# A LayerNorm put behind the first matmul that reads it, and a shift taken from four tiles

## The chip, the cores and the metric

One core of a Trainium2 chip runs the whole program. The metric is device time in microseconds (us) of one execution; the median of the runs counts.

## What is computed

Three transformer blocks on a sequence of 256 tokens with 2048 features. The change touches the seam of the second block (attention) and the third (retention). Cut to that, the reference is:

```python
# attention block: x is 256 x 2048, ALPHA = 2 ** 0.5
y = attention_out @ attn_w_out                   # 2048 x 2048
x = layer_norm(ALPHA * x + y, ln_gain[0], ln_bias[0])
# retention block reads the normed x
proj = x @ ret_w_in                              # q, k, v, gate of 8 heads
...
x = layer_norm(ALPHA * x + retention_out @ ret_w_out, ln_gain[1], ln_bias[1])

def layer_norm(x, gain, bias):
    mu = mean(x); var = mean((x - mu) ** 2)      # over the 2048 features
    return (x - mu) * rsqrt(var + eps) * gain + bias
```

## The kernel before

**Layout and arithmetic.** Activations lie transposed: a tile holds 128 features by 256 tokens, and sixteen tiles hold x. TensorE (PE) multiplies in a 32-bit format of reduced precision (fp32r), so each operand is split in a high and a low half. An activation tile is 128 x 512: columns 0 to 255 (`x[:, :T]`) the high half, columns 256 to 511 the low half. Of the weights, ScalarE (ACT) makes the high half `wh` (L374) and VectorE (DVE) the low half `wl` (L387), one unit of 128 x 1024 at a time, four buffers each. `next_unit` (L391) takes the next unit at the start of its eight (m, k) steps, issues `wh` three units ahead and `wl` two units ahead. SyncE loads the weights from HBM.

**A T job** (`job_T`, L416) makes four output tiles of 128 x 256 (or two), each in a PSUM bank of its own. A step (m, k) is two products, L449 (high weights on both halves, 512 columns) and L450 (low weights on the high half, 256 columns); with `one=True` it is three of 256 columns (L446, L447, L450), and all lands in one half of the bank. After the last k of an m it calls `evac(m, ps[m])`. With `tail=2` the last two units go m by m, so that the four results come apart; with `tail=1` all four come in the last four steps. An N job (`job_N`, L455) makes results with tokens on the partitions.

**Order of the work.** The program's order on each engine is fixed when it is built. A small scheduler (`Sched`, L274) holds generators, called tasks. Each step of a job adds its nominal 325 ns (`S.adv`), and each 650 ns is a tick: a task that has yielded n is resumed n ticks later and puts its next instructions in the queues there. `S.drain(t)` puts all the rest of a task in at once. Each engine takes its queue in order.

**PSUM banks.** `st()` (L407) hands out banks in turn. During the attention output jobs there are six (four of tag `st`, and `sx0`, `sx1`); after `more_banks(pm, 0)` (L1701) there are the four of tag `st`. The first retention job takes all four, and the job behind it (values of head 0, an N job) takes the first two of the same four again.

**The seam.** Four attention output jobs mm = 0 to 3 (L1587, L1632) give tiles 4 mm to 4 mm + 3. `ev_res` (L1370) adds both halves of the result to `xr[k]`, which holds ALPHA x, and calls `LN.add(k)`. Class `LN` (L1259):
- for k < 8, POOL (GpSimd) sums the tiles to `lnc`; after tile 7 the task `shift` (L1290) takes the mean over these features from all sixteen tiles (L1297, two of three on POOL, one on DVE), first from 8 to 15, then each of 0 to 7 with its `stat`;
- `stat(k)` (L1314): ACT squares the tile (L1321), POOL adds it to a running sum (L1322), and POOL or DVE adds the square to another (L1324);
- `ev_res` drains the shift before it touches a tile k >= 8, which is at the end of job mm = 2;
- `sums` (L1339): small products that sum over the partitions; `finish` (L1346): mean, variance, reciprocal root on DVE (three steps by `rsqrt`, L488), and two products (L1359, L1367) that spread scale (`rm`) and offset over the partitions.

After job mm = 3 all tasks are drained, `finish` is run, and the task `apply0` (L1637) norms tile after tile: times scale (L1643, POOL), plus offset (L1644, DVE), times gain plus bias to the high half (L1647, ACT) and to a full copy `lny` (L1649 on POOL for odd tiles, L1651 on ACT for even ones), and the low half as their difference (L1655, DVE). The first retention job (L1691, `rqk`: q and k of head 0, `tail=1`) reads these tiles `x3[k]`, and so does every later job of the block. Its results are added up by `ev_rqk` (L1680). Then the constants `c4` are loaded by POOL's queue (L1705), and the task `task_rope` (L1748) rotates q and k beside the value job. During job mm = 1 the task `decay` (L1596) computes the decays of the eight heads, with some fifty small DVE operations. The second LayerNorm (`ln1`, L1852) uses the same class behind the retention output.

## Time and profile before

| | us |
|---|---|
| median of 3 runs | 2308.82 |
| lowest and highest | 2308.04 and 2324.27 |
| the profiled execution | 2322.28 |
| its span (first to last instruction) | 2320.5 |
| mean granted TensorE clock in it | 0.991 of full |

The timelines below are of the profiled execution, in us from the start of its span. Engines are PE (matmul), DVE (VectorE), ACT (ScalarE), POOL (GpSimd). A clock of 1.00 is 2.4 GHz, 0.50 is 1.2 GHz.

### The profile page before, as it was taken

The numbers are of one execution on the slowest core, as the hardware profiler recorded it, in microseconds if no ns is written. First come the engines' busy times: TensorE is split into PE (matmuls) and PEld (weight loads), VectorE is DVE, ScalarE is ACT, GpSimd is POOL, SyncE is SP. The second block draws the span as 40 slices with busy tenths as digits, with TensorE's granted clock in tenths as the row PEclk, the third lists the DMA queues.
The fourth block names the chain that finished last, engine by engine and source line by source line (L and its number), as shares of the span: only waits on it lengthen the run. The fifth ranks groups of instructions, "written<-read, shape, count | busy, mean of one in ns | idle before, by whom it ended". The sixth has DMA issues, their size and how long they took to land.

```text
span 2320.5 us, 33510 instructions
## 1 busy us (share of the span) xinstructions
PE 2276.0 (98%) x12755; PEld 1963.9 (85%) x12755; DVE 1532.2 (66%) x2372; ACT 1141.5 (49%) x1690; POOL 414.8 (18%) x406
## 2 busy tenths in 40 slices
PE   8999999999999999999999999999999999999997
PEld 7877888888888888888888888888888888888887
DVE  6666697655555555555558898777677676776464
ACT  5457545544443344444445556455444544446343
POOL 2224331111100011110012222650000000001061
PEclk9999999999999999999999999989999999999998
DMA  7643455565565566666555454444655555556553
GB/s 251 227 150 112 122 187 180 195 190 187 182 192 188 177 189 189 188 185 191 183 190 181 146 156 153 156 168 160 185 168 175 179 172 187 169 173 189 188 168 114
DMA packets 114657, 408.55 MB, mean 176 GB/s; under 512 B 12882, under 2 KB 15186, under 8 KB 114368
## 3 DMA queue, kind: packets, MB, share of 16 engines
q1 hardware_dynamic: 113184, 400.80, 54.9%
q0 software_dynamic: 1168, 5.53, 0.7%
q8 instruction: 100, 1.64, 0.3%
q14 instruction: 61, 0.50, 0.1%
q10 hardware_dynamic: 144, 0.08, 0.0%
HBM read 404.24 MB, written 4.21 MB: 176 GB/s over the span
## 4 chain that ended last, share of the span: by engine, by line
PE 83%; DVE 5%; POOL 3%; issue 2%; ACT 1%; DMA 0%; POOLq 0%; ACTq 0%; DVEq 0%
PE st L449 41%; PE st L450 22%; PE st L473 5%; PE st L474 4%; PE st L475 4%; DVE wl L387 2%; POOL xr L1297 1%; PE mO L1809 1%; PE st L446 1%; PE st L447 1%; PE mA L854 1%; PE mS L1782 0%; POOL lnq L1324 0%; POOL lny L1649 0%; PE mO L835 0%
## 5 line engine op out<-in xcount | busy, mean ns | idle before, releaser
L387 DVE TENSOR_TENSOR wl<-wf,wh 128x1024 fp32r<-128x1024 f32 (+1 forms) x750 | 949.5, 1275 | 301.1 <-ACT wh L374 299.8
L374 ACT ACTIVATE wh<-wf 128x1024 fp32r<-128x1024 f32 (+1 forms) x750 | 788.4, 1055 | 698.9 <-PE st L449 440.9
L449 PE MATMUL st<-xA,wh 128*128 128x512 f32 x2144 | 768.3, 402 | 8.0 <-DVE xA L514 6.7
L450 PE MATMUL st<-xA,wl 128*128 128x256 f32 x2272 | 640.5, 282 | 2.8 <-DVE wl L387 2.8
L449 PE MATMUL st<-xB,wh 128*128 128x512 f32 x1536 | 548.7, 400 | 4.6 <-DVE xB L1655 2.1
L449 PEld LDWEIGHTS st<-xA,wh 128*128 128x128 f32 x2144 | 404.4, 189 | 107.5 <-DVE xA L514 6.7
L450 PEld LDWEIGHTS st<-xA,wl 128*128 128x128 f32 x2272 | 432.0, 190 | 4.2 <-DVE wl L387 4.1
L450 PE MATMUL st<-xB,wl 128*128 128x256 f32 x1536 | 432.0, 281 | 0.0
L449 PEld LDWEIGHTS st<-xB,wh 128*128 128x128 f32 x1536 | 290.4, 189 | 75.5 <-DVE xB L1655 3.2
L450 PEld LDWEIGHTS st<-xB,wl 128*128 128x128 f32 x1536 | 291.8, 190 | 1.1
L449 PE MATMUL st<-act,wh 128*128 128x512 f32 x704 | 248.8, 399 | 0.0
L450 PE MATMUL st<-act,wl 128*128 128x256 f32 x704 | 197.7, 281 | 0.0
L474 PE MATMUL st<-wl,xB 128*128 128x512 f32 x448 | 174.8, 390 | 1.0 <-DVE wl L387 1.0
L473 PE MATMUL st<-wh,xB 128*128 128x512 f32 x448 | 175.4, 392 | 0.0
L475 PE MATMUL st<-wh,xB 128*128 128x512 f32 x448 | 174.5, 389 | 0.0
L449 PEld LDWEIGHTS st<-act,wh 128*128 128x128 f32 x704 | 132.3, 188 | 33.1
L663 DVE TENSOR_TENSOR evs<-st,evt 128x256 f32<-128x256 f32 x110 | 46.2, 423 | 149.9 <-ACT evt L661 149.8
L450 PEld LDWEIGHTS st<-act,wl 128*128 128x128 f32 x704 | 133.0, 189 | 0.0
L1210 POOL TENSOR_TENSOR evs<-evs,R 128x256 f32<-128x256 f32 x44 | 32.4, 737 | 487.3 <-DVE evs L663 487.3
L1753 POOL TENSOR_TENSOR rm<-qkr,c 128x512 f32<-128x512 f32 x16 | 32.5, 2032 | 456.7 <-DVE qkr L1687 451.7
L474 PEld LDWEIGHTS st<-wl,xB 128*128 128x128 f32 x448 | 84.2, 188 | 17.9 <-DVE wl L387 1.9
L475 PEld LDWEIGHTS st<-wh,xB 128*128 128x128 f32 x448 | 84.1, 188 | 17.8
(426 smaller groups left out, 2604.8 us busy)
## 6 DMA issues: line engine op xcount, KB each, us to landing
wf<-in_w_c SPq DMA_DIRECT2D x264, 512.0 KB, 4.2
wf<-in_w_e SPq DMA_DIRECT2D x256, 512.0 KB, 3.9
wf<-in_w_d SPq DMA_DIRECT2D x112, 512.0 KB, 3.6
wf<-in_w_a SPq DMA_DIRECT2D x84, 512.0 KB, 3.8
wf<-in_w_b SPq DMA_DIRECT2D x32, 512.0 KB, 4.0
xr<-in_xT SPq DMA_DIRECT2D x16, 256.0 KB, 5.4
wf<-in_w_a SPq DMA_DIRECT2D x5, 420.0 KB, 4.1
dr<-d POOLq DMA_DIRECT2D x1, 2048.0 KB, 9.7
```

What stands on the lines that cost most here:

```text
L374: ACT.activation(wh[q][:, :n], wf[q][:, :n], AF.Copy)
L387: V.tensor_tensor(wl[q][:, :n], wf[q][:, :n], wh[q][:, :n].bitcast(F32), OP.subtract)
L446: PE.matmul(ps[m][:, :T], hv[:, cs], x[:, :T], start=kk == 0, stop=False)
L447: PE.matmul(ps[m][:, :T], hv[:, cs], x[:, T:], start=False, stop=False)
L449: PE.matmul(ps[m], hv[:, cs], x, start=kk == 0, stop=False)
L450: PE.matmul(ps[m][:, :T], lv[:, cs], x[:, :T], start=False, stop=kk == K - 1)
L473: PE.matmul(p, xh, h[:, o:o + n], start=kk == 0, stop=False)
L474: PE.matmul(p, xh, l[:, o:o + n], start=False, stop=False)
L475: PE.matmul(p, xl, h[:, o:o + n], start=False, stop=kk == K - 1)
L663: V.tensor_tensor(s, p[:, :T], t, OP.add)
L1210: G.tensor_tensor(s, s, R2, OP.mult)
L1753: G.tensor_tensor(m, x[:, ::-1], rsn.rearrange("p (a t) -> p a t", a=2), OP.mult)
```

## The change

**The norm moves behind the first retention job.** As soon as the statistics of tile k are issued, the new task `gain(k)` makes a tile `xg[k]` of 516 columns: high half of `xr[k]` times gain (ACT), four columns `cgb[k]` with gain and bias in halves (POOL), and the low half (DVE). `rqk` of head 0 multiplies these (`ext=True`): 260, 256 and 258 columns a step, so that each result holds also the sums of the weights times gain and times bias. `head`, `sums`, `finish` and the norming of all tiles become one task `apply0`, which starts with the job and has six ticks ahead of its first product. `ev_first` drains `apply0`, and then gives scale, offset and bias to the result. All copies `lny` go to ACT; of the products with the scale four go to DVE. `sums` is called once in place of three times.

**The shift comes from four tiles** (`NS = 4`), is begun ahead of job mm = 1 (for `ln1` behind mm = 0), and yields after each subtraction; `stat` starts two ticks later and is a task of its own for each tile. `ev_res` drains the shift from k = 4 on.

**Smaller edits.** mm = 3 has no longer `one=True`, nor extra weight buffers (`alt`) for its last two units. The normed tiles lie in other buffers (`NT`, and `GT` for the tiles of 516 columns); `c4` and the rest follow.

```diff
+GT = [f"B{k}" for k in range(6, 16)] + [f"A{k}" for k in range(6)]
+NT = [f"A{k}" for k in range(6, 16)] + [f"B{k}" for k in range(6)]
...
+                if ext:
+                    PE.matmul(ps[m][:, :T + 4], hv[:, cs], x[:, :T + 4], start=kk == 0, stop=False)
+                    PE.matmul(ps[m][:, :T], hv[:, cs], x[:, T + 4:], start=False, stop=False)
+                    PE.matmul(ps[m][:, :T + 2], lv[:, cs], x[:, :T + 2], start=False, stop=kk == K - 1)
+                    if kk == K - 1:
+                        evac(m, ps[m])
+                    S.adv(340)
+                    continue
...
         def shift(self):
-            yield 6
+            yield 5
...
-            for k in [*range(8, 16), *range(8)]:
-                (V if k % 3 == 2 else G).tensor_tensor(xr[k], xr[k], self.c, OP.subtract)
-                if k < 8:
+            n = 0
+            for k in [*range(self.NS, 16), *range(self.NS)]:
+                (V if n % 3 == 2 else G).tensor_tensor(xr[k], xr[k], self.c, OP.subtract)
+                n += 1
+                yield 1
+                if k < self.NS:
+                    S.add(self.stat(k))
                     yield 2
-                    yield from self.stat(k)
...
         def stat(self, k):
+            yield 2
...
+            if self.done:
+                yield 1
+                yield from self.done(k)
...
+    def gain(k):
+
+        if k >= 10:
+            yield 4
+        x = newg(k)
+        g = lng[0][:, k:k + 1]
+        ACT.activation(x[:, :T], xr[k], AF.Copy, scale=g)
+        G.tensor_copy(x[:, T:T + 4], cgb[:, k])
+        yield 2
+        V.scalar_tensor_tensor(x[:, T + 4:], xr[k], g, x[:, :T].bitcast(F32), OP.mult, OP.subtract)
+        xg.t[k] = x
+
+    def gain_by(k):
+        xg.by[k] = S.add(gain(k))
+        if k == 15:
+            tap.append(S.add(apply0()))
+        yield 1
...
-    for mm in range(1, 4):
-        job_T(take(), og, ev_res(ln0, mm), 2, q3 if mm == 3 else None, one=mm == 3)
-    S.drain_all()
-    rm = ln0.finish()
-    x3 = XS(S)
...
     def apply0():
-        for z in range(4):
-            (G if z else V).tensor_tensor(xr[z], xr[z], rm[z > 0], OP.mult)
+
+        yield 6
+        ln0.head()
+        ln0.sums(ln0.s, ln0.q, True)
+        yield 1
+        yield from ln0.finish()
+        rm = ln0.rm
+        yield 1
+        for z in range(2):
+            G.tensor_tensor(xr[z], xr[z], rm[1], OP.mult)
         pend = []
         for k in range(16):
-            if k + 4 < 16:
-                G.tensor_tensor(xr[k + 4], xr[k + 4], rm[1], OP.mult)
+            if k + 2 < 16:
+                (V if k % 4 == 1 else G).tensor_tensor(xr[k + 2], xr[k + 2], rm[1], OP.mult)
             V.tensor_tensor(xr[k], xr[k], rm[2], OP.add)
...
+            ACT.activation(y, xr[k], AF.Identity, scale=lng[0][:, k:k + 1], bias=lnb[0][:, k:k + 1])
             pend.append((k, x, y))
-            while len(pend) > (0 if k == 15 else 1 if k < 3 else 2):
+            while len(pend) > (0 if k == 15 else 1):
...
-            yield 1 if k < 8 else 2
-
-    tap = S.add(apply0())
+            yield 1 + k % 2
+
+    ln0.begin()
+    for mm in range(1, 4):
+        job_T(take(), og, ev_res(ln0, mm), 2)
+    while len(xg.by) < 16:
+        for t in list(S.tasks):
+            S.step(t)
...
+    def ev_first(m, p):
+
+        w, s = m // 2, m % 2
+        if s == 0:
+            qkr[(0, w)] = xa_tile("qkr", (P, 2, T))
+        S.drain(tap[0])
+        gb = small(2)
+        V.tensor_reduce(gb, p[:, T:T + 4].rearrange("p (a b) -> p b a", a=2), AX.X, OP.add)
+        q = qkr[(0, w)][:, s]
+        V.tensor_tensor(q, p[:, :T], ln0.rm[1], OP.mult)
+        V.scalar_tensor_tensor(q, ln0.rm[2], gb[:, 0:1], q, OP.mult, OP.add)
+        ACT.activation(q, q, AF.Identity, bias=gb[:, 1:2])
...
-    j = take()
-    job_T(j, x3, ev_rqk(0, 0, xa_tile))
+    job_T(take(), xg, ev_first, ext=True)
...
     for mm in range(4):
         job_T(take(), og, ev_res(ln1, mm), 2, one=mm == 3)
+        if mm == 0:
+            ln1.begin()
```

## Rows read from the trace of the kernel before

**Rows 1.** The page, busy time, share of the span and instructions of each engine.

```profile
PE 2276.0 (98%) x12755; PEld 1963.9 (85%) x12755; DVE 1532.2 (66%) x2372; ACT 1141.5 (49%) x1690; POOL 414.8 (18%) x406
```

**Rows 2.** The table by stretch: the stretch and its length in us, then busy us (and instructions) of PE, its weight loads, DVE, ACT and POOL, then the granted clock, the DMA share and GB/s.

```profile
1500.00:1510.00 10.00, 6.29 (x34) 5.79 (x34) 5.33 (x4) 5.54 (x9) 9.92 (x11) 0.69 0.38 109
...
1526.48:1561.08 34.60, 29.44 (x149) 24.77 (x148) 28.19 (x61) 22.89 (x38) 22.10 (x24) 0.80 0.29 92
...
1535.60:1541.20 5.60, 5.55 (x17) 4.49 (x18) 4.03 (x8) 3.62 (x8) 5.60 (x8) 0.50 0.00 0
...
2230.00:2240.00 10.00, 9.23 (x51) 7.37 (x49) 3.72 (x3) 5.23 (x9) 8.98 (x10) 1.00 0.48 155
```

**Rows 3.** The list of waits of PE: who waited for whom, us in total, times, the longest.

```profile
PE st L446 <- ACT wh L374: 2.8, 1, 2.8
...
PE st L449 <- DVE xB L1655: 2.1, 1, 2.1
```

**Rows 4.** The timeline of PE in and behind job mm = 2: start us, us, engine, line, instruction, and in brackets the idle time before it and who ended it.

```profile
1501.64 0.28 PE L450 MATMUL st<-xA,wl 128*128 128x256 f32 x1
...
1504.69 0.58 PE L446 MATMUL st<-xA,wh 128*128 128x256 f32 x1 [2.77 <-ACT wh L374]
...
1510.65 0.31 PE L446 MATMUL st<-xA,wh 128*128 128x256 f32 x1
...
1511.03 0.28 PE L446 MATMUL st<-xA,wh 128*128 128x256 f32 x1
...
1511.39 0.28 PE L446 MATMUL st<-xA,wh 128*128 128x256 f32 x1
```

**Rows 5.** The timeline of ACT in the same stretch, same columns.

```profile
1495.63 1.04 ACT L374 ACTIVATE wh<-wf 128x1024 fp32r<-128x1024 f32 x1
...
1501.79 1.03 ACT L1321 ACTIVATE lnt<-xr 128x256 f32<-128x256 f32 x3 [1.79 <-POOL xr L1297]
...
1503.60 1.99 ACT L374 ACTIVATE wh<-wf 128x1024 fp32r<-128x1024 f32 x2
```

**Rows 6.** The timelines of PE (its first product of job mm = 1) and of DVE, during job mm = 1, and one subtraction of the shift in mm = 2.

```profile
1450.68 0.47 PE L449 MATMUL st<-xA,wh 128*128 128x512 f32 x1
...
1462.40 1.23 DVE L387 TENSOR_TENSOR wl<-wf,wh 128x1024 fp32r<-128x1024 f32 x1
...
1464.71 3.49 DVE L387 TENSOR_TENSOR wl<-wf,wh 128x1024 fp32r<-128x1024 f32 x3
...
1483.17 0.95 DVE L1297 TENSOR_TENSOR xr<-xr,lnc 128x256 f32<-128x256 f32 x1
```

**Rows 7.** The timeline of PE from the end of job mm = 3 to the first product of the first retention job.

```profile
1525.07 0.50 PE L1343 MATMUL pcs<-ones,lns 128*128 128x1 f32 x4
...
1525.88 0.36 PE L446 MATMUL st<-xA,wh 128*128 128x256 f32 x1
...
1526.20 0.28 PE L450 MATMUL st<-xA,wl 128*128 128x256 f32 x1
...
1531.45 1.22 PE L1359 MATMUL lpb<-lndg,ones 128*128 128x256 f32 x2 [3.04 <-ACT lndg L1362]
...
1532.46 1.06 PE L1367 MATMUL lpn<-lndg,ones 128*128 128x256 f32 x2
...
1535.65 0.80 PE L449 MATMUL st<-xB,wh 128*128 128x512 f32 x1 [2.12 <-DVE xB L1655]
```

**Rows 8.** The timelines of DVE (five rows) and ACT (four rows) in `finish` and `apply0`, and two rows of the table of groups from 1533.6 to 1557.2 (line, engine, operation, shapes, count, busy us, mean ns, idle us before and its releaser).

```profile
1528.45 0.16 DVE L1350 TENSOR_SCALAR sm<-pcs 128x2 f32<-128x2 f32 x1 [1.50 <-PE pcs L1343]
...
1531.00 0.29 DVE L1364 TENSOR_SCALAR lndg<-ident,sm 128x128 f32<-128x128 f32 x1
...
1546.42 0.95 DVE L1655 TENSOR_TENSOR xB<-lny,xB 128x256 fp32r<-128x256 f32 x1
...
1553.12 0.42 DVE L1655 TENSOR_TENSOR xB<-lny,xB 128x256 fp32r<-128x256 f32 x1
...
1556.77 0.43 DVE L1655 TENSOR_TENSOR xB<-lny,xB 128x256 fp32r<-128x256 f32 x1 [0.38 <-POOL lny L1649]
...
1534.11 0.60 ACT L1647 ACTIVATE xB<-xr,vec 128x256 fp32r<-128x256 f32 x1
...
1547.80 0.60 ACT L1647 ACTIVATE xB<-xr,vec 128x256 fp32r<-128x256 f32 x1 [0.79 <-DVE xr L1644]
...
1548.30 0.59 ACT L1651 ACTIVATE lny<-xr,vec 128x256 f32<-128x256 f32 x1
...
1548.80 1.05 ACT L374 ACTIVATE wh<-wf 128x1024 fp32r<-128x1024 f32 x1
...
L1655 DVE TENSOR_TENSOR xB<-lny,xB 128x256 fp32r<-128x256 f32 x16 | 9.9, 621 | 2.1 <-POOL lny L1649 1.9
...
L1643 POOL TENSOR_TENSOR xr<-xr,lnrm 128x256 f32<-128x256 f32 x12 | 9.8, 836 | 0.0
```

**Rows 9.** The timelines of DVE (the first evacuation of the first retention job) and of PE (the start of the value job, and two products of it that waited).

```profile
1559.70 0.42 DVE L1687 TENSOR_TENSOR qkr<-st,evt 128x256 f32<-128x256 f32 x1 [0.23 <-ACT evt L1686]
...
1561.08 0.40 PE L473 MATMUL st<-wh,xB 128*128 128x512 f32 x1
...
1570.12 0.50 PE L474 MATMUL st<-wl,xB 128*128 128x512 f32 x1 [0.43 <-DVE wl L387]
...
1573.74 0.50 PE L474 MATMUL st<-wl,xB 128*128 128x512 f32 x1 [0.61 <-DVE wl L387]
```

More of the change, by code (lines that the diff above doesn't have):

```diff
@@ L414, in more_banks, with job_T @@
         banks["n"] = 0
-    def job_T(j, xs, evac, tail=1, alt=None, raw=None, one=False):
+    def job_T(j, xs, evac, tail=1, raw=None, one=False, ext=False):
         K, nt, kc = len(j["rows"]), len(j["tiles"]), j["kc"]
@@ L427, in job_T @@
                 kn = min(kc, K - k0)
[L428 removed]
+                h, l = next_unit(tail > 1 and cc == nch - 1)
                 hv = h[:, :kn * nt * P].rearrange("p (k m) -> p k m", k=kn)
@@ L1260, in body, with __init__ @@
         tag = "m"
-        def __init__(self, pool, x, pair):
+        NS = 4
+        def __init__(self, pool, x, pair, done=None):
             self.base = pool
@@ L1266, in __init__ @@
             self.c, self.s, self.q = t("lnc"), t("lns"), t("lnq")
-            self.task = None
-            self.x, self.pair = x, pair
+            self.x, self.pair, self.done = x, pair, done
             self.tpre = S.add(self.pre())
@@ L1288, in pre, with begin, head @@
                 yield 1 + k % 2
+        def begin(self):
+            self.task = S.add(self.shift())
         def shift(self):
-            yield 6
+            yield 5
             pb = self.pp.tile([P, 512], F32, name="lp", tag=self.tag)
             PE.matmul(pb[:, :T], ones, self.c, start=True, stop=True)
-            ACT.activation(self.c, pb[:, :T], AF.Copy, scale=1.0 / (8 * P))
+            ACT.activation(self.c, pb[:, :T], AF.Copy, scale=1.0 / (self.NS * P))
             yield 1
-            for k in [*range(8, 16), *range(8)]:
-                (V if k % 3 == 2 else G).tensor_tensor(xr[k], xr[k], self.c, OP.subtract)
-                if k < 8:
+            n = 0
[5 more added lines that the diff above has]
+                    S.add(self.stat(k))
                     yield 2
-                    yield from self.stat(k)
         def add(self, k):
-            if k < 8:
-                if k == 0:
-                    G.tensor_copy(self.c, xr[k])
-                else:
-                    G.tensor_tensor(self.c, self.c, xr[k], OP.add)
-                if k == 7:
-                    self.task = S.add(self.shift())
-            else:
-                S.add(self.stat(k))
+            if k >= self.NS:
+                S.add(self.stat(k))
+            elif k == 0:
+                G.tensor_copy(self.c, xr[k])
+            else:
+                G.tensor_tensor(self.c, self.c, xr[k], OP.add)
+        def head(self):
+            self.ps = self.pp.tile([P, 512], F32, name="pcs", tag=self.tag)
+            for tt in range(2):
+                PE.matmul(self.ps[:, 2 + tt:3 + tt], ones, deps, start=tt == 0, stop=False,
+                          skip_group_check=True)
         def stat(self, k):
+            yield 2
             if k == 0:
@@ L1317, in stat @@
                 ACT.activation(self.q, xr[k], AF.Square)
-                return
-            if k < 14:
+            elif k < 14 or self.done:
                 sq = self.base.tile([P, T], F32, name="lnt", tag="lnt", bufs=3)
@@ L1324, in stat @@
                 (G if k < 12 else V).tensor_tensor(self.q, self.q, sq, OP.add)
-                if k == 11:
-                    self.ps = self.pp.tile([P, 512], F32, name="pcs", tag=self.tag)
-                    for tt in range(2):
-                        PE.matmul(self.ps[:, 2 + tt:3 + tt], ones, deps, start=tt == 0, stop=False,
-                                  skip_group_check=True)
+                if self.done:
+                    pass
+                elif k == 11:
+                    self.head()
                 elif k == 13:
@@ L1594, in body @@
     ln0.pools(q3, pm)
+    cgb = q3.tile([P, 16, 4], F32R, name="cgb")
+    for z, v in enumerate((lng[0], lnb[0])):
+        ACT.activation(cgb[:, :, z], v, AF.Copy)
+        V.tensor_tensor(cgb[:, :, 2 + z], v, cgb[:, :, z].bitcast(F32), OP.subtract)
     def decay():
@@ L1677, in xa_tile @@
         spare[0] += 1
-        return pxs.tile(list(shape), F32, name=name, tag=f"xA{spare[0] % 16}")
+        t = xtile(GT[spare[0] % 16], F32)
+        return t[:, :shape[1]] if len(shape) == 2 else t.rearrange("p (a t) -> p a t", a=shape[1])
+    def ev_first(m, p):
[9 more added lines that the diff above has]
+        ACT.activation(q, q, AF.Identity, bias=gb[:, 1:2])
     def ev_rqk(h, m0, mk):
@@ L1855, in body @@
         job_T(take(), og, ev_res(ln1, mm), 2, one=mm == 3)
+        if mm == 0:
+            ln1.begin()
     S.drain_all()
-    rm = ln1.finish()
+    run(ln1.finish())
+    rm = ln1.rm
     for k in range(16):
```

59 lines of the change are left out of this document (30 added, 29 removed).

## The prediction, written before the changed kernel had run

> **What bounds the kernel now.** I read the page's busy shares first: TensorE (PE) is busy nearly all of the span [rows 1], so a change is worth the time in which PE stands still or runs at its lower clock. The table by stretch [rows 2] was next, and it shows three such places in reach of this change. The list of PE's waits [rows 3] names who ended the idle time, and the timelines of PE and of the engine named [rows 4, 5, 7 to 9] give the length.
>
> Place one, in the third attention output job (mm=2): PE stops after the product at 1501.64, restarts at 1504.69, waits again, and runs at half clock until 1510.65 [rows 4]. ACT's queue made it: the weight copy behind this wait sat from 1495.63 to 1503.60 behind squares of the LayerNorm that waited for POOL [rows 5]. Place two, the norm itself: the last product of the job is at 1526.20 and ends at 1526.48 (call this E), the first product of the retention job starts at 1535.65 [rows 7], and then runs at 0.50 of the clock [rows 2]. Place three is a small copy of place one in the last LayerNorm, 2230 to 2240, PE 9.23 of 10.00 [rows 2].
>
> The reader should also see a fourth thing. In the 34.6 us from E to the second retention job DVE is busy 28.2 us and ACT 22.9 us [rows 2]. What these two do there is normalise x and split it for all later jobs. The change doesn't take this work away, it takes PE's first job out from behind it.
>
> **Place one: shift from four tiles.** PE lost from 1501.76 to 1510.65, 8.9 us, for 24 products that take 0.12 us each at full clock (three of them from 1511.03 to 1511.39): 2.9 us. So 6.0 us are lost [rows 4]. In the change the shift starts in mm=1, the sixteen subtractions are spread by one tick each, and a square is issued two ticks after its result. ACT then waits for POOL only in the tail of mm=1, where I count 15 POOL operations in some 8.5 us; at 0.84 us each [rows 8] POOL is late by 4 us at most, against the 8 us that broke it before [rows 5]. I take the whole gain: **-6.0 us** (ends 0 and -6.0).
>
> **New cost in mm=1.** DVE runs the decay task there and is already late: the low halves of units 5, 6, 7 follow in the order 1462.40 and three together at 1464.71 [rows 6]. PE starts the job at 1450.68 and takes 2.9 us a unit (eight steps of 0.36), so it wants unit 5 at 1465.1 and unit 6 at 1468.0; unit 5 is there at 1463.6, unit 6 some 1.2 us after 1464.71, at 1465.9. The slack is 1.5 and 2.1 us. Ahead of unit 6 now come three of the five DVE subtractions, at 0.43 to 0.95 us (2.0 in all at the middle) [rows 6, 8], the two small ones for the columns (0.3), and POOL beside two weight subtractions (an estimate of 0.5 each, by what the 0.43 us subtraction loses to POOL at its worst): 3.3 us against 2.1. I take **+1.2 us** (ends 0 and +3.5, the latter with a clock drop as in place one).
>
> **Sums.** Of the three calls of sums two are gone, and the one left moves behind E: **-0.8 us** before E (1525.07 to 1525.88 [rows 7]); its return is in the walk below. mm=3 goes from three 256-column products a step to one of 512 and one of 256, and the first retention job the other way round (260, 256, 258 columns): 768 columns either way but for six, so I count nothing; the ends are 0.3 us on either side.
>
> **Place two, walked from E.** The gained sums xg[0] to xg[11] are ready, so PE goes straight on. DVE still owes evacuation 15, two additions of squares, two low halves (13 and 12) and then the low half of the job's second unit: 0.9 + 4 x 0.45 + 1.1 = 3.8 us, where PE wants it at 8 x 0.36 = 2.9; PE waits 0.9. The head and sums stand at tick 7 (13 steps of 0.36 us, plus the wait): E+6, and end at E+7.2. Then DVE: thirteen small operations, 2.55 us (1528.45 to 1531.00 [rows 8]), with one low half of weights (1.1) between them, diagonal at E+11; ACT's half E+11.6; PE, which by then stands at this product, waits 0.5 and needs 0.5 (1.0 at half clock, 1531.45 to 1532.46 [rows 7]); another low half on DVE, the second diagonal, ACT's copy of the scale: E+13.5; POOL's first product and DVE's first addition: the loop over sixteen tiles begins at **E+14.8**. In the kernel before it begins at 1534.11, E+7.6 [rows 8].
>
> How long is the loop? ACT now makes both copies of each tile, 0.5 us apart (1547.80, 1548.30, 1548.80 [rows 8]): 16 x 1.0, and four weight copies of 1.05: 20.2 us is its floor. Before, the loop took 1534.11 to 1557.2, 23.1 us [rows 8]. DVE needs about 19 us, with a wait for ACT in every pair of tiles. I take 21.5, near the floor, because POOL's eight copies leave: **E+36.3**. The ends are 20.2 and 26.9 (below).
>
> On the same point the Trainium skill, SBUF — State Buffer, section Who interferes with whom, says that a DVE instruction with two SBUF inputs contends with a GpSimd instruction that reads SBUF. The trace agrees: the subtraction at L1655 takes 0.62 us on the mean beside POOL's products of 0.84 [rows 8], and 0.43 in its last copy, without them. By that rule the loop is shorter than before with eight POOL copies fewer, and the rival of a slow loop is less likely.
>
> Now who waits. The loop is paced by ticks, 1.5 a tile from tick 16, and the job has 31 before its first result: tile 10 is reached. ev_first drains the rest, tiles 11 to 15, ahead of its own operations on DVE. And the second job (values, head 0) writes its first product into the same PSUM bank that the first result occupies: four banks rotate, the job before filled all four. In the kernel before that bank was read from 1559.70, and PE came at 1561.08 without a wait [rows 9]. In the change PE is done with the first job at E + 23.0 (64 x 0.36) + 0.9 + 1.2 + 1.5 = E+26.6, and the bank is free when DVE has finished the loop and the reduce and the product of ev_first (0.6): **E+37**. PE stands for 10 us. Before it started the second job at E+34.6. So what was to be gained at the norm is given back one job later: **+2.4 us**.
>
> The idle of 10 us is followed by the lower clock, as after the norm before: 17 products in 5.6 us at 0.50 [rows 2], where 17 of a mean 0.18 take 3.0: **+2.6 us** (the old one of the same size is inside E+34.6). In the second job PE waited 0.4 and 0.6 us for DVE at 1570.12 and 1573.74 [rows 9]; a slower start spares these, and the rotation behind it, which starts later, may cost up to 2: I take 0 (ends -1 and +2).
>
> **Place three** goes as place one does, and has neither decay nor extra columns: **-0.8 us**.
>
> Sum: -6.0 + 1.2 - 0.8 + 2.4 + 2.6 - 0.8 = -1.4 us. The profiled execution took 2322.28 us, with a span of 2320.5; so 2320.9. The median of the runs is 2308.82, 13.5 us lower, and the terms are waits that don't depend on that difference: 2308.8 - 1.4 = 2307.4, said as **2307 us**. A measurement of this kernel can tell about 1% from no change, 23 us.
>
> **Rivals.** (1) The gap closes: DVE and ACT finish before PE is done with the first job. Then PE goes on at E+26.6, 8.0 us before E+34.6, with no second stop and no lower clock: -6.0 + 1.2 - 0.8 - 8.0 - 0.8 = -14.4, 2294 us. For it: PE's next operands are ready at E. Against: ACT alone has 16 us of copies [rows 8] after E+14.8, so only a part of it can come. (2) The slow loop, the other side: the loop decides alone when PE restarts, so every microsecond in it is one in the time. It breaks even at 21.5 + 1.4 = 22.9 us, just under what it took before. In the stretch from 1546.42 to 1553.12 four tiles took 6.7 us [rows 8], 1.68 each; at that rate it takes 26.9 us, +5.4 over the sum: +4.0, 2313 us. For it: three DVE operations and two ACT operations a tile with weights between. Against: fewer POOL operations. (3) The shift does not end the stall of mm=2: POOL's rush in the tail of mm=1 holds ACT's squares for longer than the weights have slack. Then -6.0 stays out: +4.6, 2313 us. For it: the same ACT order; against: 4 us of lateness, not 8.
>
> **Chances.** Forecast 45%, its own range 2303 to 2312 (loop 20.2 to 24, mm=1 0 to 3). Gap closed or mostly so 20%, slow loop 22%, stall kept 13%. The range: 2294 to 2317, from the closed gap to a slow loop with the rotation late. No case reaches 23 us: all stalls together, places one to three with the lower clock, are some 19 us, so faster by over 1% gets 3%; slower by over 1% would take two rivals and a clock drop in each job, 3%; within 1% 94%.
>
> **What would show it.** PE's idle time between the attention output and the first retention job under 1.5 us in all; a new wait of about 10 us of PE at the first product of the value job, released by DVE in ev_first; granted clock 0.50 right after it; PE full between the start of mm=2 and its end; the last of the sixteen subtractions about 36 us after the last attention product. Wrong would be: no such wait at the value job (rival 1), a wait over 13 us there (2), ACT weight copies 8 us apart in mm=2 (3).

## The result: 1.0069 times the time before, and the profile after

The changed kernel takes 2325.79 us (median of 11 runs, 2324.96 to 2328.41), the kernel before 2308.82 us beside it: ratio 1.0069, 95% interval [1.0055, 1.0082]. It is slower by 17.0 us, where 1.4 us less was predicted, and it lies above the range (2294 to 2317). One thing has to be known to read any time here: runs of the kernel before fall into two groups, 107 of its 147 runs in this study at 2305.1 to 2312.2 (median 2308.5, called pace F below), 40 at 2318.6 to 2324.3 (median 2321.6, pace S), and none between.

The profiled execution of the changed kernel took 2327.35 us, its span is 2325.3; that of before, 2322.28 and 2320.5, was of pace S. So the two traces differ by only 4.8 us of the 17. I read the page first, then the table by stretch and the list of PE's waits. The page's busy shares, to be read against [rows 1]:

```profile
PE 2273.4 (98%) x12739; PEld 1961.3 (84%) x12739; DVE 1551.6 (67%) x2406; ACT 1153.8 (50%) x1717; POOL 409.3 (18%) x405
```

The table by stretch, columns as in [rows 2], whose four stretches these answer (E, the end of attention output, is 1526.75 now), with one in job mm=1 ahead of them:

```profile
1463.00:1473.00 10.00, 8.44 (x40) 6.86 (x40) 9.28 (x33) 1.08 (x3) 2.62 (x6) 0.87 0.39 111
...
1500.00:1510.00 10.00, 10.00 (x59) 8.71 (x58) 8.21 (x13) 6.77 (x12) 7.67 (x11) 1.00 0.56 181
1526.75:1565.70 38.95, 25.77 (x209) 25.08 (x208) 33.23 (x72) 28.38 (x50) 14.29 (x19) 0.90 0.44 145
1565.70:1571.30 5.60, 5.60 (x13) 4.43 (x14) 5.50 (x12) 3.94 (x6) 2.95 (x2) 0.50 0.09 11
...
2230.00:2240.00 10.00, 10.00 (x59) 8.73 (x59) 4.51 (x4) 3.48 (x4) 0.00 (x0) 1.00 0.66 199
```

Place one is gone, and so is place three (10.00, before 9.23). Place one doesn't lie in mm=2, where the prediction and [rows 4] put it, but in mm=3: its products are those of L446 and L447, which only a job with `one=True` has, and counted back from E, 64 steps a job, mm=3 starts at 1495.04 in the kernel before and at 1504.10 in the changed one. The whole of mm=3, before and after:

```profile
1495.04:1526.48 31.44, 27.45 (x209) 26.75 (x207) 19.00 (x22) 13.92 (x21) 18.95 (x20) 0.89 0.54 185
```

```profile
1504.10:1526.75 22.65, 22.65 (x132) 19.79 (x131) 16.48 (x22) 10.88 (x17) 9.04 (x12) 1.00 0.60 187
```

But a stop has come in mm=1 (PE 8.44, clock 0.87), and from E to the value job's first product it is 38.95 us now, before 34.60. Who is waited for stands in the list of PE's waits, to be read against [rows 3], whose two entries it no longer has:

```profile
PE st L475 <- DVE xB L1750: 12.3, 1, 12.3
...
PE st L452 <- DVE wl L384: 5.8, 5, 2.5
```

The timeline of PE gives the places: one row that serves below as a mark (A, the last product that waits for an x tile of attention output; before it is 1444.69), the stops in mm=1, the first retention job and the value job [rows 6, 7, 9].

```profile
1445.88 0.50 PE L451 MATMUL st<-xA,wh 128*128 128x512 f32 x1 [0.80 <-DVE xA L521]
...
1462.53 0.58 PE L452 MATMUL st<-xA,wl 128*128 128x256 f32 x1 [2.45 <-DVE wl L384]
...
1471.64 0.39 PE L452 MATMUL st<-xA,wl 128*128 128x256 f32 x1 [1.28 <-DVE wl L384]
...
1530.81 0.39 PE L442 MATMUL st<-xg,wl 128*128 128x258 f32 x1 [0.91 <-DVE wl L384]
...
1565.70 0.76 PE L475 MATMUL st<-wh,xA 128*128 128x512 f32 x1 [12.27 <-DVE xB L1750]
```

The timeline of DVE in mm=1 (four rows) and from the loop's first addition to the first result (four):

```profile
1456.60 0.66 DVE L1660 TENSOR_TENSOR sm<-sm 128x16 f32<-128x16 f32 x1
1457.29 0.67 DVE L1661 TENSOR_SCALAR sm<-sm 128x16 f32<-128x16 f32 x1
...
1460.66 1.82 DVE L384 TENSOR_TENSOR wl<-wf,wh 128x1024 fp32r<-128x1024 f32 x1
...
1467.15 0.17 DVE L1663 TENSOR_SCALAR sm<-sm 128x16 int32<-128x16 f32 x1
...
1540.59 0.42 DVE L1702 TENSOR_TENSOR xr<-xr,lpn 128x256 f32<-128x256 f32 x1 [1.32 <-POOL xr L1697]
...
1564.73 0.43 DVE L1710 TENSOR_TENSOR xB<-lny,xB 128x256 fp32r<-128x256 f32 x1 [0.57 <-ACT lny L1706]
1565.07 0.15 DVE L1748 TENSOR_REDUCE sm<-st 128x2 f32<-128x4 f32 x1
1565.14 0.41 DVE L1750 TENSOR_TENSOR xB<-st,lnrm 128x256 f32<-128x256 f32 x1
```

and beside the first of them the timelines of POOL and of ACT in mm=1:

```profile
1455.80 7.97 POOL L1314 TENSOR_TENSOR xr<-xr,lnc 128x256 f32<-128x256 f32 x10 [2.16 <-ACT lnc L1310]
```

```profile
1471.92 0.22 ACT L1677 ACTIVATE sm<-sm 128x16 f32<-128x16 f32 x1 [9.79 <-DVE sm L1676]
```

The reader is to see ten subtractions of the shift back to back on POOL, and beside them the decay's operations on 128x16 numbers at 0.66 us each on DVE; once POOL is done they take 0.17, what the same code takes throughout mm=1 in the kernel before:

```profile
1455.14 0.18 DVE L1606 TENSOR_TENSOR sm<-sm 128x16 f32<-128x16 f32 x1
1455.35 0.17 DVE L1607 TENSOR_SCALAR sm<-sm 128x16 f32<-128x16 f32 x1
```

The weights' low halves wait in DVE's queue behind them, ACT's logarithm waits 9.79 us for the decay, the weight copies wait behind the logarithm, and PE stops.

### The profile page after: what moved, and what is told of

Its sections match the earlier page's. It is cut to its first block, busy times and chain, and to the rows that moved or that the text cites. A ratio compares the mean times of both kernels' runs of the same rounds, so it can differ in the third digit from the quotient of the medians.

```text
span 2325.3 us, 33536 instructions
## 1 busy us (share of the span) xinstructions
PE 2273.4 (98%) x12739; PEld 1961.3 (84%) x12739; DVE 1551.6 (67%) x2406; ACT 1153.8 (50%) x1717; POOL 409.3 (18%) x405
## 4 chain that ended last, share of the span: by engine, by line
PE 83%; DVE 6%; issue 2%; ACT 2%; POOL 1%; DMA 1%; POOLq 0%; ACTq 0%; DVEq 0%
PE st L451 41%; PE st L452 21%; PE st L475 5%; PE st L476 5%; PE st L477 5%; DVE wl L384 2%; PE mO L1882 1%; PE st L448 1%; PE st L449 1%; PE mA L865 1%; PE mS L1855 0%; PE mO L846 0%; POOL xr L1314 0%; ACT wh L374 0%; DMA wf<-in_w_b 0%
## 5 line engine op out<-in xcount | busy, mean ns | idle before, releaser
L451 PE MATMUL st<-xA,wh 128*128 128x512 f32 x2688 | 961.1, 399 | 8.0 <-DVE xA L525 6.7
L452 PE MATMUL st<-xA,wl 128*128 128x256 f32 x2712 | 764.5, 282 | 6.1 <-DVE wl L384 5.8
L451 PEld LDWEIGHTS st<-xA,wh 128*128 128x128 f32 x2688 | 507.4, 189 | 127.7 <-DVE xA L525 6.7
L451 PE MATMUL st<-xB,wh 128*128 128x512 f32 x992 | 353.9, 398 | 3.4 <-DVE evs L674 2.6
L452 PE MATMUL st<-xB,wl 128*128 128x256 f32 x1032 | 289.7, 281 | 0.0
L451 PEld LDWEIGHTS st<-xB,wh 128*128 128x128 f32 x992 | 186.4, 188 | 48.8 <-DVE evs L674 3.2
L452 PEld LDWEIGHTS st<-xB,wl 128*128 128x128 f32 x1032 | 194.1, 188 | 0.2
L475 PE MATMUL st<-wh,xA 128*128 128x512 f32 (+2 forms) x352 | 135.6, 385 | 12.3 <-DVE xB L1750 12.3
L476 PE MATMUL st<-wl,xA 128*128 128x512 f32 (+2 forms) x352 | 132.4, 376 | 0.7 <-DVE wl L384 0.7
L477 PE MATMUL st<-wh,xA 128*128 128x512 f32 (+2 forms) x352 | 132.5, 377 | 0.0
L475 PE MATMUL st<-wh,xB 128*128 128x512 f32 x288 | 113.7, 395 | 0.0
L477 PE MATMUL st<-wh,xB 128*128 128x512 f32 x288 | 112.8, 392 | 0.0
```

The source lines that it names most:

```text
L451: PE.matmul(ps[m], hv[:, cs], x, start=kk == 0, stop=False)
L452: PE.matmul(ps[m][:, :T], lv[:, cs], x[:, :T], start=False, stop=kk == K - 1)
L475: PE.matmul(p, xh, h[:, o:o + n], start=kk == 0, stop=False)
L476: PE.matmul(p, xh, l[:, o:o + n], start=False, stop=False)
L477: PE.matmul(p, xl, h[:, o:o + n], start=False, stop=kk == K - 1)
```

## The experiments

**Where the other 12 us are.** Before any edit, the traces: counting products from the start, the two paces part only between some 440 and 1140 us, in the feed-forward stage, where PE never waits. One stretch of it, in the profiles of before (S), of before run again (F) and of after; columns as in [rows 2]:

```profile
600.00:700.00 100.00, 100.00 (x568) 86.67 (x567) 53.39 (x65) 46.55 (x64) 11.15 (x14) 1.00 0.62 188
```

```profile
600.00:700.00 100.00, 100.00 (x579) 88.32 (x578) 56.55 (x73) 46.70 (x63) 11.18 (x14) 1.00 0.61 188
```

```profile
600.00:700.00 100.00, 100.00 (x571) 87.15 (x570) 53.28 (x64) 46.37 (x64) 11.13 (x14) 1.00 0.62 190
```

Full granted clock in all three, yet 568, 579 and 571 products. Of the pair of products that each weight tile takes, it is the one of 512 columns that differs; from the table of groups, 520 to 1100 us, before (S) and before (F), mean ns behind the bar:

```profile
L449 PE MATMUL st<-act,wh 128*128 128x512 f32 x513 | 181.4, 399 | 0.0
```

```profile
L449 PE MATMUL st<-act,wh 128*128 128x512 f32 x546 | 189.4, 391 | 0.0
```

8 ns on each of some 1640 such products are 13 us, the distance of the two groups. All 11 runs of the changed kernel are in one group.

For the seam the time is split at marks of PE's timeline, in us: A as above, V the first product of the value job, O the first product into mO behind it, and the end of the span. The feed-forward lies ahead of A, so its pace is not in these columns. Each row is one profile, and the scatter has to be known: before, x0_before, b_pad516, b_off512 and b_prew32 run the same instructions behind A and spread from 873.7 to 876.5 from A to the end, b_pre32 stands apart at 869.7. The fast median of the kernel before, too, moves from 2307.7 to 2309.5 between the groups of runs. A difference of 2 us between two kernels is therefore read below only where rows show what makes it.

| profiled run | pace | A to V | V to O | O to end | A to end |
|---|---|---|---|---|---|
| before | S | 116.39 | 28.77 | 730.65 | 875.81 |
| b_prew32 | S | 115.76 | 28.83 | 729.15 | 873.74 |
| b_pad516 | S | 115.86 | 28.96 | 731.68 | 876.50 |
| after | S | 119.82 | 30.07 | 729.53 | 879.42 |
| a_decay3 | S | 114.65 | 29.93 | 729.43 | 874.01 |
| a_evfirst | S | 112.63 | 34.35 | 729.49 | 876.47 |
| a_both | S | 107.41 | 34.35 | 729.54 | 871.30 |
| a_pre32 | S | 120.04 | 29.37 | 729.61 | 879.02 |
| a_own_both | S | 107.08 | 43.34 | 727.29 | 877.71 |
| a_own2_both | S | 107.81 | 43.05 | 726.37 | 877.23 |
| b_shift4 | S | 114.90 | 29.06 | 727.38 | 871.34 |
| x0_before | F | 116.06 | 28.70 | 729.11 | 873.87 |
| b_off512 | F | 116.19 | 28.50 | 729.16 | 873.85 |
| b_pre32 | F | 114.41 | 29.04 | 726.21 | 869.66 |
| a_own | F | 120.18 | 35.37 | 726.36 | 881.91 |
| b_shift4_decay3 | F | 112.81 | 28.80 | 727.18 | 868.79 |
| b_pre32_s4d3 | F | 111.41 | 29.43 | 724.54 | 865.38 |

**x0_before: the kernel before again, no edit.**

> The kernel before, unchanged. Its profiled execution took 2322.3 us, its median run 2308.8, so 13.5 us of the 17 us that the change costs aren't in the comparison of the two traces. Theory A (the trace of before fell on a slow case of the same program): a second profile near 2309 us has no stop of PE of 2.8 us in the third attention output job, or keeps the full clock behind some of its stops. Theory B (profiling itself costs the 13 us): the second profile is again near 2322 us and shows the same stops as the first.

2308.07 us (10 runs; 8 near 2307.8, 2 near 2320.0), profiled at 2308.07. The trace has the stop of mm=3 and the gap at the norm as in [rows 3], so neither theory was right: the difference is not in the seam, and profiling costs nothing. It is the pace.

**a_decay3: the decay two jobs later.**

```
-    S.add(decay())
     for mm in range(1, 4):
+        if mm == 3:
+            S.add(decay())
         job_T(take(), og, ev_res(ln0, mm), 2)
```

> The changed kernel with the decay task begun at the fourth attention output job in place of the second. Theory 1 (DVE's small decay operations wait for POOL's subtractions of the shift, 0.67 us each in place of 0.17, and ACT's logarithm and the weights behind it wait with them): the three waits of PE in the second job (2.45, 0.28, 1.28 us) and the lower clock behind the first go, 5 to 7 us less than the changed kernel, 2319 to 2321. Rival 2 (the five subtractions on DVE make the waits, wherever decay stands): 0 to 2 us.

2321.74 us (2320.69 to 2322.53), 4.1 under after. From A to E it takes 75.69 us, after 80.87 and before 81.79. By jobs, from the first product of each to that of the next (mm=3 to E), in us:

| profiled run | mm=1 | mm=2 | mm=3 |
|---|---|---|---|
| before | 22.69 | 22.97 | 31.44 |
| after | 29.69 | 23.85 | 22.65 |
| a_decay3 | 23.24 | 22.75 | 25.00 |

With the decay out of mm=1 its stop goes although the shift's subtractions stay there, so rival 2 is out: the collision costs the change 7.5 us in mm=1 and mm=2. 2.4 of them come back where the decay stands now, in mm=3, so that 5.2 are gained up to E and 4.1 in the time, a little under the forecast. The wait for the low halves goes from 5.8 us to

```profile
PE st L452 <- DVE wl L384: 3.4, 3, 1.5
```

**a_evfirst: the drain at the first results no longer runs the loop to its end.**

```
-        S.drain(tap[0])
+        while not hasattr(ln0, "rm"):
+            S.step(tap[0])
```

> The changed kernel with the first retention job's results taken out ahead of the norming of tiles 11 to 15: ev_first steps the task only until scale and offset are there, and the rest of it follows behind the four results. Theory 1 (PE waits 12.3 us at the value job for a PSUM bank behind those tiles): the wait falls to 3 to 6 us, and 6 to 9 us go, 2317 to 2320; then waits for tiles 11 to 15 and for weights may come. Rival 2 (DVE and ACT are late anyway, and the wait comes back at the next weights): under 3 us.

2323.63 us (2322.77 to 2325.32), 2.2 under after; A to the end 3.0 less. The rows of PE say where the rest went:

```profile
1557.16 0.77 PE L475 MATMUL st<-wh,xA 128*128 128x512 f32 x1 [4.97 <-DVE xB L1751]
...
1568.22 0.50 PE L476 MATMUL st<-wl,xA 128*128 128x512 f32 x1 [2.57 <-DVE wl L384]
```

The bank comes free 7.2 us sooner (A to V 112.63, after 119.82), which shows that the drain held it. 4.3 us of that are lost again between V and O (34.35, after 30.07): the loop's tiles and the next weights share DVE and ACT whichever is issued first. The work is only moved, as the rival had it.

**b_shift4: the kernel before with the new shift alone.** `ln0.begin()` and `ln1.begin()`, the shift from four tiles and its spread statistics; the norm, its sums and the 512-column tiles stay as before.

> The kernel before with only the shift from four tiles (and the tasks for it), the norm where it was. Theory 1 (the shift beside decay costs more than the stop in the third job did): slower than before by 2 to 8 us. Rival 2 (the loss is all at the value job): faster by 4 to 6 us, since the stop in the third job goes.

2305.82 us (7 runs near 2305.3, 3 near 2317.5), ratio 0.9985 [0.9959, 1.0012]; 3.2 under before at pace F, 4.1 at S. Not slower, as I had expected from the collision in mm=1. The collision is there (1460 to 1470: PE 7.83, clock 0.83), and the stop of mm=3 that goes is worth a little more (A to E 79.98, before 81.79).

```profile
1460.00:1470.00 10.00, 7.83 (x33) 6.30 (x34) 9.35 (x28) 0.54 (x1) 3.99 (x6) 0.83 0.36 105
```

**b_pad516: the kernel before with the wider tiles alone.**

```
+    def xtile(t, dt):
+        if t in GT:
+            return pxs.tile([P, 516], dt, ...)[:, :512]
```

> The kernel before, with one thing of the change: the sixteen x tiles that the change widens are allocated with 516 columns (2064 B of a partition) and used through their first 512; no instruction is another. Theory P (the change's missing 12 us are the pace of the feed-forward products, and the wider tiles set that pace by moving what lies in SBUF): at 2318 to 2322, ratio 1.004 to 1.006, in nearly every run, with 115 to 117 products in 20 us of the feed-forward stage in place of 117.4, and no other stage longer. Rival C (the pace is a matter of the run, or of the change's instructions, not of the tiles): as before, 2306 to 2310 in most runs and 2318 to 2322 in a quarter, ratio 0.999 to 1.002.

2323.37 us (2321.52 to 2325.06), ratio 1.0051 [1.0033, 1.007]: all ten at pace S, 570 products in the stretch. No instruction differs from before. The widths of sixteen tiles alone put it 13.9 us above the kernel before at pace F beside it (median 2309.5), level with the two runs of the kernel before that were at pace S there (2323.4 and 2323.9). Whether it takes just these 16 B a tile isn't shown: with 576 columns the tiles don't fit in the kernel before, and the two changed kernels with that width (a_pad576, ab_pad576) have no time either.

```profile
600.00:700.00 100.00, 100.00 (x570) 87.16 (x569) 53.65 (x66) 46.69 (x64) 11.12 (x14) 1.00 0.62 189
```

**b_off512 and a_own: what the widening moves.** The first leaves 512 B empty behind the x tiles. The second is the changed kernel with the wide tiles allocated in the norm's pool: `return q3.tile([P, 516], F32R, name="xg", tag=f"xg{k}")` in `newg`, 512 columns in `xtile`.

> The kernel before with 512 B of each partition left empty between the x tiles and what is allocated behind them (the feed-forward's act tiles and scratch among it): the x tiles stay where they were, 2048 B apart, and all behind them moves by as much as in the kernel after. One memset of it is the only added instruction. Theory Q (the pitch of the x tiles against the weights sets the pace of the feed-forward products): as before, 2306 to 2310 in most runs, 117.4 products in 20 us of that stage, ratio 0.999 to 1.001. Rival S (the shift of what lies behind the x tiles does it): 2320 to 2324 in nearly all runs, 115 to 117 products, ratio 1.004 to 1.007.

2309.31 us, 7 runs near 2307.9 and 3 near 2322.5, ratio 1.0003 [0.9974, 1.0032]: as before. Moving what lies behind the x tiles by 512 B doesn't fix the pace.

> The kernel after with the sixteen tiles of 516 columns allocated in the pool of the norm's stage, which has the room, and all x tiles 512 columns wide again as before; no instruction is another. Theory P (the wider tiles cost 11 to 13 us by the pace of the feed-forward products, the seam the rest): 2312 to 2315, ratio 1.001 to 1.003, 117.4 products in 20 us of the feed-forward stage, the seam as in the kernel after. Rival (the pace hangs on something else that the change does): 2324 to 2327.

9 runs, 4 near 2317.1 and 5 near 2329.1, profiled at 2317.00 with 578 products in the stretch: the two paces are back, so the widening in the shared pool had fixed the slow one.

```profile
600.00:700.00 100.00, 100.00 (x578) 88.16 (x578) 56.00 (x72) 47.10 (x64) 11.19 (x14) 1.00 0.62 190
```

At equal pace the changed kernel in this form is slower than before by 8.6 us (F) and 7.5 (S), more than I had expected. Part of it is this pool's own: the timeline of POOL shows that the transfer of the next stage's constants, issued at 1550.40 in the kernel after, whose E is 12.2 us later, waits until the first results have left the norm's rows:

```profile
1556.68 0.58 POOL L1778 DMA_DIRECT2D c<-in_c  x1 [18.46 <-DVE xB L1751]
```

DVE then stands for 5.33 us (its rope, waiting for POOL's), with a low half of weights queued behind it: V to O 35.37.

**a_own_both and a_own2, a_own2_both.** a_own with both seam edits; then a_own and a_own_both with an unused 8 KB tile ahead of the last wide one.

> The kernel of the run before this one, with the decay begun at the third tile of attention output and with the drain at the first results stepping the norm's loop only until the rest of its rows exist. By the terms measured one by one (12 for the tiles, 4.1 and 2.2 less than after): 2306 to 2309, ratio 0.998 to 1.000. If the two seam edits meet in the same wait and don't add: 2309 to 2312.

10 runs, 4 near 2310.3 and 6 near 2325.1: at pace F 1.8 above before and 6.8 under a_own, where 6.3 were forecast for the two, so they do add. That it lies in the range given for the other case comes of a_own, which is slower than it was taken to be.

> The kernel after with its sixteen wide tiles in the pool of the norm's stage, as in the earlier run, and an unused tile of 8 KB ahead of the last of them, so that the constants of the next stage no longer wait for memory in which the norm's rows lie. Theory: the constants' transfer is issued some 5 us earlier and the value job's weights come as in the kernel after; from the last wait of PE for an input of attention output to the end 877 to 880 us (before 873.9 at the fast pace, 875.8 at the slow one; after 879.4), so 2311 to 2314 at the fast pace and 2323 to 2327 at the slow one. Rival (the time behind the norm hangs on something else in that pool): 881 to 883, 2315 to 2319 and 2328 to 2330 as in the earlier run.

2315.31 us over nine runs (2313.74 to 2318.30), all at pace F; a tenth, the profiled one, took 7924.27 us and is left out of the times. It is 6.8 us above before, and 1.8 under a_own, no more than the scatter. The order can still be read in the trace of that tenth: the constants' transfer waits there for the same operation on the first results as in a_own, so the 8 KB didn't free it.

> The kernel of the run before this one with the decay begun at the third tile of attention output and the drain at the first results stepping the loop only until the rest of its rows exist. By the terms measured one by one (5.4 and 3.0 off the stretch from attention output to the end): 868 to 872 us there, 2302 to 2306 at the fast pace and 2315 to 2319 at the slow one, level with the shift and the later decay alone (2302 to 2304 and 2313 to 2315), so that the norm's move itself brings nothing. Rival (the norm's move brings what it removes, the wait for the normed tiles): 2295 to 2300 at the fast pace.

10 runs, 7 near 2310.8 and 3 near 2323.2. No better than a_own_both, so the expectation failed: the tile of 8 KB doesn't help. V to O is 43.05 us (a_own_both 43.34), and POOL's timeline and PE's say why: the transfer now waits for the last tile of the norm's loop, which the second edit has put behind the first results (in a_both, with the tiles where the change has them, it is issued at 1544.02 without a wait). DVE stands 5.81 us for the rope behind it, and PE for the low half behind that:

```profile
1564.69 0.58 POOL L1782 DMA_DIRECT2D c<-in_c  x1 [17.95 <-DVE xB L1711]
```

```profile
1576.36 0.79 PE L476 MATMUL st<-wl,xA 128*128 128x512 f32 x1 [6.72 <-DVE wl L384]
```

The rival, 2295 to 2300, failed by more.

**b_shift4_decay3: the shift and the later decay, the norm ahead as before.** b_shift4 with the diff of a_decay3: the decay begins with mm=3, the fourth job of the attention output (the expectations from here on say third tile).

> The kernel before with the shift from four tiles alone (the norm still ahead of the first retention job, 512-column tiles) and the decay begun at the third tile of attention output. If the collision of POOL's subtractions with the decay's small operations is what ate the gain of the shift in the kernel after: 2299 to 2304, ratio 0.996 to 0.998. If the decay's place doesn't matter where the norm stays ahead: 2304 to 2308, as with the shift alone.

10 runs, 4 near 2303.3 and 6 near 2313.8: at equal pace 5.2 (F) and 7.8 (S) under before. The stretch that stood at clock 0.83 in b_shift4:

```profile
1460.00:1470.00 10.00, 10.00 (x60) 8.81 (x59) 9.65 (x7) 5.93 (x8) 9.92 (x7) 1.00 0.63 204
```

From A to E it is 8.0 us shorter than before (73.80, before 81.79), but 4.4 of them come back ahead of V: E to V is 39.01 us, before 34.60. The statistics end behind E here, and PE waits for them:

```profile
1507.14 0.64 PE L1356 MATMUL pcs<-ones,lns 128*128 128x1 f32 x4 [1.73 <-POOL lns L1333]
```

**b_pre32, b_prew32, a_pre32: 32 bytes.** An unused tile of 32 B a partition, between weights and x tiles of before, ahead of both, and between weights and x tiles of after.

> The kernel before with 32 B of each partition left empty ahead of the x tiles, so that all x tiles and all behind them lie 32 B further from the weight tiles, still 2048 B apart; one memset of these bytes is the only added instruction. Theory Q1 (what counts is where an x tile begins against a multiple of some larger size, not the pitch): the slow pace in nearly every run, 2320 to 2324, 115 to 117 products in 20 us of the feed-forward stage. Theory Q2 (it is the pitch, by which the sixteen tiles stand each at another place): both paces as before, 2306 to 2310 in most runs and 2319 to 2323 in the others.

2306.26 us (2304.57 to 2308.49), ratio 0.9985 [0.9973, 0.9997], all ten runs at pace F, 579 products in the stretch: both theories wrong. Beside them the kernel before was at pace S in only 4 of 25, so ten could be chance; b_pre32_s4d3 below, with the same 32 B, has another ten of ten, where 8 of 29 were. With these twenty, 32 B there fix the fast pace. They also shorten A to the end by 4.2 us (869.66, x0_before 873.87) with no instruction changed there: the feed-forward is not the only stage that the placement may reach. One profile shows this, and nothing here says how.

> The kernel before with 32 B of each partition left empty ahead of the weight tiles, so that weights, x tiles and all behind them lie 32 B further, each as before against the others; one memset is added. Theory R (the place of the x tiles against the weight tiles decides): both paces as before, 2305 to 2311 in most runs and 2319 to 2324 in the others. Rival T (the address itself decides): the fast pace in nearly every run, 2304 to 2309, as with 32 B between the weights and the x tiles.

2323.13 us (2319.79 to 2327.51), ratio 1.0057 [1.0039, 1.0074], all ten slow, 568 products. Both wrong again: it is neither the x tiles' place against the weights (as before here) nor their own address (that of b_pre32). The stretch in b_pre32 and in b_prew32:

```profile
600.00:700.00 100.00, 100.00 (x579) 88.67 (x578) 56.90 (x72) 46.79 (x64) 10.95 (x14) 1.00 0.61 186
```

```profile
600.00:700.00 100.00, 100.00 (x568) 86.89 (x567) 52.64 (x63) 46.73 (x64) 11.13 (x14) 1.00 0.61 190
```

> The kernel after with 32 B of each partition left empty between the weight tiles and the x tiles; one memset is added. Theory U (the pitch of the widened tiles fixes the slow pace wherever they begin): 2324 to 2329, 115 to 117 products in 20 us of the feed-forward stage. Rival V (the 32 B give the fast pace here too): 2311 to 2316, 117.4 products.

2323.97 us (2322.34 to 2324.66), 573 products in the stretch: U holds for the time, with a pace a little nearer to the fast one.

**a_both: both seam edits at the change's own placement.**

> The kernel after, its tiles as in the change, with the decay begun at the third tile of attention output and the drain at the first results stepping the norm's loop only until the rest of its rows exist. If the two add: 2325.8 less 4.1 and 2.2, 2319 to 2320; from the last wait of PE for an input of attention output to the end 870 to 872 us (before 875.8 at the slow pace). If they meet in one wait: 2321 to 2323, 873 to 875 us.

2318.31 us (2317.60 to 2322.42), A to the end 871.30: the two add, 7.5 less than after, at its pace. That is 5.1 under b_pad516, whose tiles and pace are the same; b_shift4_decay3, without the norm's move, gains 7.8 at pace S. So the move of the norm, even repaired, adds nothing that these runs show.

**b_pre32_s4d3: the parts that gained, put together.** b_shift4_decay3 with the 32 B of b_pre32.

> The kernel before with 32 B of each partition left empty between the weight tiles and the x tiles, with the shift from four tiles and with the decay begun at the third tile of attention output; the norm stays ahead of the first retention job. If the parts add: 2306.3 less 5, 2300 to 2303 in every run, ratio 0.995 to 0.997. If the 32 B have already what the two seam edits gain: 2304 to 2307.

2300.31 us (2299.50 to 2302.18), ratio 0.9955 [0.9936, 0.9973], every run at pace F. It beats both kernels: 8.2 us under before at the fast pace, 25.5 under after.

## Why the prediction was wrong, step by step

Of the 17.0 us between the medians, 13 to 14 are the pace: the two groups lie 13.1 apart (2321.6 less 2308.5), and b_pad516, with the tiles alone, lies 13.9 above pace F of the kernel before beside it. Some 3 are left to the change's instructions, which fits the +3.6 from A to the end below.

- **The step that failed** is in the sum: "The median of the runs is 2308.82, 13.5 us lower, and the terms are waits that don't depend on that difference". I took the 13.5 us for a constant and never asked what it was. It was a second pace of the longest stage, the profile sat in it, and a part of the change decides it. The widening of sixteen tiles was priced nowhere: it has no row of its own, and I counted instructions only. b_pad516 (2323.4) shows that it alone makes the kernel miss the range. Without some 13 us of pace the time would lie near 2312, inside it, though with +3.6 where -1.4 was added up.
- **mm=1 was mis-sized**: +1.2 us with an end of +3.5, measured +7.0 (29.69, before 22.69) and +0.9 in mm=2; without the collision (a_decay3) +0.6 and -0.2. I let POOL slow DVE's large subtractions and left the decay's small ones at 0.17 us. Eleven of those between 1455.89 and 1465.7 took some 0.5 us more each beside POOL, 5.5 us of lateness. The Trainium skill, SBUF — State Buffer, section Who interferes with whom, has the rule, though not this price: besides a DVE instruction with two SBUF inputs beside a GpSimd one that reads SBUF, a tensor_scalar too can run in a mode that takes the port pair shared with GpSimd, and whichever issues first then holds the pair for its whole instruction, while the other blocks. The trace agrees: TENSOR_SCALAR at 0.67 us beside subtractions of 0.80 each (7.97 for ten), and TENSOR_TENSOR likewise. The slack was misread as well: the product at 1450.68 in [rows 6] is that of the fourth step of mm=1 and not its first, which is at 1449.38; three steps, some 1.1 us, go off each slack.

```profile
1449.38 0.40 PE L449 MATMUL st<-xA,wh 128*128 128x512 f32 x1
```

- **Place one was right in its mechanism, but in another job and larger**: it lies in mm=3, which takes 31.44 us before and 22.65 after, -8.8 where -6.0 and the sums' -0.8 were predicted. Of **place three**, -0.8, the wait is gone from the list of PE's waits (0.77 us before); O to the end, 1.1 less in after, doesn't show it: the kernel before itself has 730.65 and 729.11, and the wide tiles cost time here too. The five profiled kernels that have them in the shared pool take 729.4 to 729.6 from O to the end, the three that have them in the norm's pool 726.4 to 727.3.
- **The walk from E**: PE waits 0.91 at the second unit (predicted 0.9); the loop's first addition is at E+13.8 (E+14.8); its last subtraction ends at 1565.16, E+38.4 (E+36.3): 24.6 us, not 21.5. ACT's floor was right (it is busy 20.32 us of the 24.57), but it waits for DVE besides, twice 1.1 us behind low halves of weights that take 1.76 and 1.77 us beside POOL's products with the scale, 1.22 once these have ended. POOL's eight copies had left, but ten of its products had stayed:

```profile
1543.05 1.76 DVE L384 TENSOR_TENSOR wl<-wf,wh 128x1024 fp32r<-128x1024 f32 x1
...
1552.57 1.22 DVE L384 TENSOR_TENSOR wl<-wf,wh 128x1024 fp32r<-128x1024 f32 x1
```

```profile
1540.52 9.93 POOL L1701 TENSOR_TENSOR xr<-xr,lnrm 128x256 f32<-128x256 f32 x10
```

```profile
1545.19 0.60 ACT L1705 ACTIVATE xA<-xr,vec 128x256 fp32r<-128x256 f32 x1 [1.11 <-DVE xr L1702]
```

- **The second stop**: its mechanism, the bank behind the drain, was right (a_evfirst), 12.27 us against 10. The start of the value job is E+38.95 against 34.60: +4.35, predicted +2.4. The clock fell to 0.50 behind it as said, and V to O is 1.3 us longer (predicted +2.6).
- In sum, from A to the end: -0.9 (A to E, predicted -5.6), +4.35, +1.3 and -1.1, together +3.6 where -1.4 was predicted. Rival 2, the slow loop, came nearest in the seam: its break-even of 22.9 us was passed, though the wait at the value job stayed under the 13 us that the prediction gave as its sign. None of the rivals had the pace. a_own's +8.6 at pace F is more than this +3.6: 2.5 of the difference lies between A and the end (881.91 less 879.42), 1.9 is the scatter of the kernel before (875.81 less 873.87), the rest is not placed.

## What to carry to other kernels

When the profiled execution and the median differ, find out where before adding terms to either: count one stage's instructions in equal stretches of two profiles. Before a tile's size is changed in a pool that a long stage uses, price its placement too, by one run with the allocation alone; where the wide tiles live only in one stage, that stage's pool may hold them. And a small DVE operation that is moved beside a burst on POOL, or a burst moved beside it, has to be priced near the length of POOL's instruction (here 0.67 us beside 0.80), not by its own (0.17).

## What the runs showed of the hardware

- The pace of the feed-forward's products depends on where tiles lie in SBUF: 579 or 568 in 100 us at granted clock 1.00, with weight loads of 189 ns in both. 32 B ahead of the x tiles gave the fast pace in ten of ten runs, and in ten more with other edits of the seam; 32 B ahead of weights and x tiles the slow one in ten of ten, sixteen tiles of 516 columns the slow one in ten of ten, 512 B behind them left it to chance as before (3 of 10 slow). Why isn't shown, nor why the unedited kernel takes now one pace, now the other (40 of 147 slow). The Trainium skill, SBUF — State Buffer, section Who interferes with whom, says that PE never waits on another engine; these runs don't show that one does, but PE's products here are not of one length.
- Within one run the pace holds throughout the stage in the kernel before (115 products in each 20 us, or 117 to 118), while with the wider tiles it drifts between 115 and 117.
- DVE operations on 128x16 numbers took 0.17 us alone and 0.65 to 0.70 beside subtractions on POOL.
